# Seven quarter products for eight in a gated linear attention layer, with values and gates of all heads ahead of the heads

## The chip, the core and the metric

The kernel runs on one core of one Trainium2 chip, with nothing on the other cores. The metric is device time in microseconds (us) of one execution, the median of several runs. A core has a matrix engine (TensorE, PE in the profile; its weight loads are PEld), VectorE (DVE), ScalarE (ACT), GpSimd (POOL) and SyncE (SP), each with an instruction queue of its own that works in order, and 16 DMA engines that serve all queues. SBUF is the on-chip memory, PSUM holds TensorE's sums in eight banks of 128 x 512 float32, DRAM lies off the core.

## What is computed

Two layers, each `x <- x + RMSNorm_post(mixer(RMSNorm_pre(x)))`, on 512 tokens of 1024 channels in float32. The first layer (a state-space branch beside a convolution branch) is not touched. The second is gated linear attention with 4 heads, keys of 256 and values of 512 channels a head, in chunks of 64 tokens:

```python
q, k, v, r, lr = jnp.split(u @ od_w_in, ...)          # 1024, 1024, 2048, 2048, 16 columns
g = jax.nn.log_sigmoid(lr @ w_gate_up + b_gate) / 16
b = cumsum of g inside each chunk
attn = where(causal, (q * exp(b)) @ (k * exp(-b)).T, 0)
o = attn @ v + (q * exp(b)) @ state                   # state carried from chunk to chunk
state = exp(b_last) * state + (k * exp(b_last - b)).T @ v
y = (rms_norm(o) * silu(r)) @ od_w_out
```

## The kernel before

**Split numbers.** Every float32 operand of a large product is held as a high part (rounded to TensorE's fp32r) and a low part (the rest), and a product is three matmuls: high x high, low x high, high x low. For weights this is done on the fly: `wlist` names blocks of 128 x 1024 (512 KB) in the order of use; `w_raw` (L113 to L120) loads the next one on SP's queue into one of three `wraw` buffers; `w_split` (L134 to L164) casts it on ScalarE (L155, `wh`, two buffers) and subtracts on VectorE (L161, `wl`, three buffers). In parts of the first layer the low part is made by ScalarE and an accumulating DMA from SBUF to SBUF on GpSimd's queue instead (L130, L131). `w_get` keeps the split one block ahead of its use. `feed()` raises the priority of such work. The order on each engine is made by the planner of the tile framework, which simulates the program with costs of its own and takes what is ready, by priority and then program order.

**A projection with tokens in rows** (`proj_mv`, `mm_mv`, L813 to L831) takes 512 output columns: 4 weight blocks, 4 token groups of 128, 8 groups of 128 channels, 3 matmuls each, 96 matmuls in all, 24 a block (L823 to L825), into four PSUM banks. A head's values are one such projection, its gate r another. Queries and keys go the other way round (`mm_st`, L198 to L201), 24 matmuls a block, 4 blocks a head.

**The second layer.** The normalised input lies in SBUF as `u1h` and `u1l`, 8 channel groups x 512 tokens. First come the values of head 0 (L1003), then the decays of all heads: eight small matmuls (L1006) with absolute value, exponential and logarithm on ScalarE (L1008, L1015), minimum, subtraction and prefix sums on VectorE (L1009, L1024, L1021), then the gate of head 0. Then for each head: queries and keys with their exponentials; values (heads 1 to 3, into the same tiles `vh`, `vl`); scores (L1109) with mask and split into `ah`, `al`; the gate (heads 1 to 3), whose SiLU (L998) stays in SBUF as `rg`; in head 2 also half of the output projection, for heads 0 and 1; then attention times values (L1144 to L1146) for four token groups, each followed by its norm (L1153 to L1156), four transposes (L1159) and a split into `oth`, `otl`. The other half of the output projection and the last norm follow (`proj_tail`).

Of the kernel before, what the change touches and what calls it, by code (L numbers as in the profile page):

```python
# [17 lines left out]
P = 128  # L18
# [33 lines left out]
def trunk(ctx: ExitStack, tc: tile.TileContext, A: dict, out: bass.AP, dbg: dict | None = None):  # L52
# [47 lines left out]
    for n in range(2):  # L100
        for j in range(4):
            wlist.append(A["w_out0"][n, 4 + j])
    for h in range(HEADS):
        wv, wr = ([A["w_vr"][o + h, j] for j in range(4)] for o in (0, 4))
        wqk = [A["w_qk"][2 * h + j] for j in range(2)] + [A["w_qk"][8 + 2 * h + j] for j in range(2)]
        wlist.extend(wv + wr + wqk if h == 0 else wqk + wv + wr)
        if h >= 2:
            for n in range(2):
                for j in range(4):
                    wlist.append((j % 2, A["w_out1"][n, (h - 2) * 4 + j]))  # L110
    wst = {"next_raw": 0, "next_split": 0, "raw": {}, "hl": {}, "low": {}}

    def w_raw():  # L113
        i = wst["next_raw"]
        if i >= len(wlist):
            return
        raw = wpool.tile([P, 1024], F32, tag="wraw", bufs=3, name=f"wraw{i}")
        SY.dma_start(raw, wlist[i][1] if isinstance(wlist[i], tuple) else wlist[i])
        wst["raw"][i] = raw
        wst["next_raw"] = i + 1  # L120
# [13 lines left out]
    def w_split(dst=None):  # L134
        i = wst["next_split"]
        while wst["next_raw"] <= i:
            w_raw()
        if i in dma_low and i not in wst["low"]:
            w_low(i, dst and dst[1])
        raw = wst["raw"].pop(i)  # L140
        h = wpool.tile([P, 1024], F32R, tag="wh", bufs=2, name=f"wh{i}") if dst is None else dst[0]
        if isinstance(wlist[i], tuple):

            l = wpool.tile([P, 1024], F32R, tag="wl", bufs=3, name=f"wl{i}") if dst is None else dst[1]
            for e in range(2):
                es_, g_ = slice(e * S, (e + 1) * S), wst["gain"][:, 2 * wlist[i][0] + e:2 * wlist[i][0] + e + 1]
                with feed():
                    SC.activation(h[:, es_], raw[:, es_], AF.Copy, scale=g_)  # L148
                    V.scalar_tensor_tensor(out=l[:, es_], in0=raw[:, es_], scalar=g_, in1=h[:, es_].bitcast(F32), op0=ALU.mult, op1=ALU.subtract)  # L149
            wst["hl"][i] = (h, l)  # L150
            wst["next_split"] = i + 1
            w_raw()
            return
        with feed():
            SC.copy(h, raw)  # L155
        if i in dma_low:
            l = wst["low"].pop(i)
        else:
            l = wpool.tile([P, 1024], F32R, tag="wl", bufs=3, name=f"wl{i}") if dst is None else dst[1]
            with feed():  # L160
                V.tensor_tensor(out=l, in0=raw, in1=h.bitcast(F32), op=ALU.subtract)  # L161
# [705 lines left out]
    for i in range(2):  # L867
# [7 lines left out]
        wlr.append((wa, wb_))  # L875
    for i in range(2):
        raw = tmp((96, S))
        for r in range(3):
            SY.dma_start(raw[32 * r:32 * r + 32], A["w_gate"][:, i * S:(i + 1) * S])
        g_ = sbt_((96, S), F32R, f"gws{i}")  # L880
        SC.copy(g_, raw)
        V.tensor_sub(g_[64:96], raw[64:96], g_[64:96].bitcast(F32))
        gws.append(g_)
    lrs = sbt_((96, S), F32R, "lrs")

# [78 lines left out]
    wst["gain"] = pa.tile([P, TT], F32, name="ngc")  # L964
    ngp = ps("cv")
    PE.transpose(ngp[:, 0:TT], ngr, ident[0:TT, 0:TT])
    V.tensor_copy(wst["gain"], ngp[:, 0:TT])
    reset = pa.tile([P, S], mybir.dt.bfloat16, name="reset")
# [10 lines left out]
    PG = ExitStack()  # L979
    pg = PG.enter_context(tc.tile_pool(name="l1g", bufs=1, side="right", reuse_waits="tile"))  # L980
    lacc = ps("cv")
    for k in range(KT):
# [9 lines left out]

    def gate(h):
        accs = proj_mv(u1h, u1l)
        rg = []
        for tt in range(TT):
            r_ = sbt_((P, S), F32, f"rg{h}{tt}")
            SC.activation(r_, accs[tt], AF.Silu)  # L998
            rg.append(r_)
        return rg  # L1000

    values(vblocks)
    az = pg.tile([P, KT, S], F32, name="az")  # L1003
    for kt in range(KT):
        gp = ps(("mm", "mm", "mm", "aux", "aux", "aux", "mm", "aux")[kt])
        PE.matmul(gp, gws[kt // 4][:, kt % 4 * P:(kt % 4 + 1) * P], lrs, start=True, stop=True)  # L1006
        bg_ = vec[:, 5, kt:kt + 1]
        SC.activation(az[:, kt, :], gp, AF.Abs, bias=bg_)  # L1008
        V.tensor_scalar(out=bcum[:, kt, :], in0=gp, scalar1=bg_, scalar2=0.0, op0=ALU.add, op1=ALU.min)  # L1009
    last = None  # L1010
    for f, kw in ((AF.Exp, dict(scale=-1.0)), (AF.Ln, dict(bias=1.0))):
        with tc.issue_after(last.ins) if last else ExitStack():
            for k0 in range(0, KT, 2):
                a_ = az[:, k0:k0 + 2, :]
                i_ = SC.activation(a_, a_, f, **kw)  # L1015
        last = i_

# [4 lines left out]

    for kt in range(KT):
        V.tensor_sub(bcum[:, kt, :], bcum[:, kt, :], az[:, kt, :])  # L1024
        if kt == 1:
            sums(0)
    rg = gate(0)
    PG.close()

    pb = L1.enter_context(tc.tile_pool(name="l1b", bufs=1, side="right", reuse_waits="tile"))  # L1030
    pq = LQ.enter_context(tc.tile_pool(name="l1q", bufs=1, side="right", reuse_waits="tile"))
    R_OFF = (0, 448, 768, 960)
# [4 lines left out]
    yp_d = dram.tile([S, D], F32, name="yp_d")  # L1037
    for h in range(HEADS):

# [43 lines left out]
        for j in range(2):  # L1083
# [3 lines left out]
            ec, es = el[j]  # L1087
            evicted = V.tensor_mul(kr[:, 0:S], acc, en[j])  # L1088
            fac = small.tile([P, 3, 2], F32, tag="fac", bufs=2, name=f"fac{h}{j}")
# [3 lines left out]
                            in1=fac.rearrange("p i a -> p (i a)").unsqueeze(2).to_broadcast([P, 6, 64]), op=ALU.mult)  # L1093
            split(kh[:, j, :], kl[:, j, :], kr)
        if h:
# [28 lines left out]
        split(ah[:, 0:S], al[:, 0:S], at.rearrange("p j t -> p (j t)"))  # L1124
        if h:
            rg = gate(h)

        if h == 2:
            for n in range(2):
                accs = proj_mv(*oa)  # L1130
                for tt in range(TT):
                    yt = tmp(name="ypc")
                    SC.copy(yt, accs[tt])
                    SY.dma_start(yp_d[tt * P:(tt + 1) * P, n * S:(n + 1) * S], yt)

        if h % 2 == 0:
            oth = pb.tile([P, KT, S], F32R, tag="oth", bufs=1, name=f"oth{h}")
            otl = bigt(F32R, f"otl{h}")
        acol = {(0, 3): 512, (0, 2): 640, (0, 1): 768, (1, 3): 896, (1, 2): 1024, (2, 3): 1152}
        for i in range(4):  # L1140
            acc = ps("aux")
            for jj in range(i + 1):
                c0 = jj * P if jj == i else acol[(jj, i)]
                PE.matmul(acc, ah[:, c0:c0 + P], vh[:, jj, :], start=(jj == 0), stop=False)  # L1144
                PE.matmul(acc, ah[:, c0:c0 + P], vl[:, jj, :], start=False, stop=False)  # L1145
                PE.matmul(acc, al[:, c0:c0 + P], vh[:, jj, :], start=False, stop=(jj == i))  # L1146
            if "o" in dbg:
# [8 lines left out]
            V.scalar_tensor_tensor(out=og, in0=acc, scalar=rr, in1=rg[i], op0=ALU.mult, op1=ALU.mult)  # L1156
            tp = ps("cv")
            for j in range(4):
                PE.transpose(tp[:, j * P:(j + 1) * P], og[:, j * P:(j + 1) * P], ident)  # L1159
            k0 = 4 * (h % 2)  # L1160
            split(oth[:, k0:k0 + 4, i * P:(i + 1) * P], otl[:, k0:k0 + 4, i * P:(i + 1) * P], tp.rearrange("p (k t) -> p k t", t=P))
        if h == 1:
            oa = (oth, otl)
    LQ.close()

# [11 lines left out]
    E1.close()  # L1177
    L1.close()
    SBP.close()
    L0.close()  # L1180
# [67 lines left out]
```

## Time and profile before

| | |
|---|---|
| median of three runs | 934.77 us (934.74 to 936.48) |
| the profiled execution | 936.94 us, of it 935.2 us span from first to last instruction |
| TensorE busy | 895.1 us, 4397 matmuls, mean granted clock 0.991 |
| VectorE, ScalarE, GpSimd busy | 645.2, 485.1, 225.0 us |
| DMA | 142.48 MB, mean 152 GB/s |
| second layer | from about 520 us on |

A row of the profile names a line of the kernel, an engine, an operation, `out<-in` by tile names, the shapes and the count. "Idle before" is the time in which the engine had nothing to do just ahead of such an instruction, with what ended it. A matmul's shown length is its latency; matmuls overlap, so the distance of their starts is what a stream of them costs. "DMA share" is the mean busy share of the 16 DMA engines, "us to landing" the time from a transfer's issue to its completion.

### The profile page before, as it was taken

Reading aid. Unit: us, or ns where it says so; the run is one execution under the profiler, and the core shown is the slowest. Engines: PE = TensorE matmul, PEld = TensorE weight load, DVE = VectorE, ACT = ScalarE, POOL = GpSimd, SP = SyncE. Lnnn points to the kernel's source line nnn. Section 1 sums busy time; section 2 is a strip of 40 time slices with the busy share of each in tenths; the row PEclk is TensorE's granted clock in tenths of the full one; section 3 lists DMA queues with packets and bytes.
Section 4 is the critical chain, followed back from the end, with each engine's and each line's share of the span. In section 5 each row is a group of like instructions: output and inputs, shape, how many; then the busy total and the mean of one; then the engine's idle time right before and its main releaser. Section 6 shows DMA issues by size and latency. Waiting matters only on the chain. (4 is left out here: it accounts for less than half of the span.)

```text
span 935.2 us, 12132 instructions
## 1 busy us (share of the span) xinstructions
PE 895.1 (96%) x4397; PEld 718.9 (77%) x4397; DVE 645.2 (69%) x1225; ACT 485.1 (52%) x699; POOL 225.0 (24%) x242
## 2 busy tenths in 40 slices
PE   5999998999999999999999979999999999999996
PEld 4876767777788877778887768888888888888885
DVE  7994999999999978822578446694384222744646
ACT  6545686877668745654444654443533243523530
POOL 2795656552041322011054000010000000000022
PEclk9999999999999999999999989999999999999999
DMA  9979987888697894298553122212221223324512
GB/s 288 253 169 228 267 208 181 196 189 203 190 255 203 204 251 135 90 243 186 173 197 113 46 67 96 85 38 77 90 90 68 83 76 136 135 90 152 208 46 90
DMA packets 54820, 142.48 MB, mean 152 GB/s; under 512 B 14245, under 2 KB 15785, under 8 KB 54761
## 3 DMA queue, kind: packets, MB, share of 16 engines
q1 hardware_dynamic: 46696, 112.36, 36.2%
q0 software_dynamic: 8064, 29.36, 17.4%
q8 instruction: 34, 0.56, 0.2%
q14 instruction: 26, 0.20, 0.1%
HBM read 94.92 MB, written 13.22 MB: 116 GB/s over the span
## 5 line engine op out<-in xcount | busy, mean ns | idle before, releaser
L155 ACT CAST wh<-wraw 128x1024 fp32r<-128x1024 f32 x114 | 119.5, 1049 | 138.5 <-PE ps_mm L824 61.9
L676 DVE SCALAR_TENSOR_TENSOR ps_cv<-h,cw,ps_cv 128x512 f32<-128x512 f32 x232 | 161.8, 746 | 2.7 <-ACT ps_cv L673 1.8
L161 DVE TENSOR_TENSOR wl<-wraw,wh 128x1024 fp32r<-128x1024 f32 x58 | 71.6, 1235 | 85.7 <-ACT wh L155 85.7
L198 PE MATMUL ps_mm<-u0h,wh 128*128 128x512 f32 x320 | 128.0, 401 | 1.2 <-ACT tmp L700 0.7
L199 PE MATMUL ps_mm<-u0l,wh 128*128 128x512 f32 x320 | 127.1, 398 | 0.0
L823 PE MATMUL ps_mm<-wh,u1h 128*128 128x512 f32 x240 | 95.6, 400 | 3.3 <-ACT wh L155 3.1
L824 PE MATMUL ps_mm<-wh,u1l 128*128 128x512 f32 x240 | 95.8, 399 | 0.3 <-DVE u1l L206 0.3
L825 PE MATMUL ps_mm<-wl,u1h 128*128 128x512 f32 x240 | 92.6, 402 | 1.7 <-DVE wl L161 1.7
L131 POOL DMA_DIRECT2D wl<-wraw x56 | 48.9, 889 | 172.1 <-ACT wl L130 155.8
L201 PE MATMUL ps_mm<-u0h,wl 128*128 128x512 f32 x320 | 82.4, 396 | 2.2 <-DMA wl<-wraw 2.2
L130 ACT ACTIVATE wl<-wraw 128x1024 fp32r<-128x1024 f32 x56 | 59.2, 1057 | 26.7 <-DMA wraw<-in_w_in_dram 16.2
L198 PEld LDWEIGHTS ps_mm<-u0h,wh 128*128 128x128 f32 x320 | 60.4, 189 | 16.0 <-ACT tmp L700 1.5
L201 PEld LDWEIGHTS ps_mm<-u0h,wl 128*128 128x128 f32 x320 | 59.5, 188 | 16.1 <-DMA wl<-wraw 3.1
L199 PEld LDWEIGHTS ps_mm<-u0l,wh 128*128 128x128 f32 x320 | 60.3, 189 | 13.3 <-issue 0.7
L1092 POOL TENSOR_TENSOR kr<-kr,fac 128x384 f32<-128x384 f32 x8 | 9.1, 1132 | 217.8 <-DVE kr L1088 122.6
L823 PEld LDWEIGHTS ps_mm<-wh,u1h 128*128 128x128 f32 x240 | 45.6, 190 | 14.2 <-ACT wh L155 3.6
L825 PEld LDWEIGHTS ps_mm<-wl,u1h 128*128 128x128 f32 x240 | 45.7, 191 | 13.0 <-DVE wl L161 2.4
L824 PEld LDWEIGHTS ps_mm<-wh,u1l 128*128 128x128 f32 x240 | 45.7, 190 | 11.0 <-DVE u1l L206 0.6
L199 PE MATMUL ps_mm<-u1l,wh 128*128 128x512 f32 x128 | 50.4, 394 | 0.0
L198 PE MATMUL ps_mm<-u1h,wh 128*128 128x512 f32 x128 | 50.3, 393 | 0.0
L149 DVE SCALAR_TENSOR_TENSOR wl<-wraw,ngc,wh 128x512 fp32r<-128x512 f32 x24 | 17.0, 747 | 39.3 <-ACT wh L148 39.3
L903 POOL TENSOR_TENSOR yp<-yp,gain 128x512 f32<-128x512 f32 x8 | 12.6, 1591 | 118.9 <-ACT junk L230 118.9
(348 smaller groups left out, 2041.9 us busy)
## 6 DMA issues: line engine op xcount, KB each, us to landing
wl<-wraw POOLq DMA_DIRECT2D x56, 512.0 KB, 6.4
wraw<-in_w_in_dram SPq DMA_DIRECT2D x40, 512.0 KB, 5.5
wraw<-in_w_out_dram SPq DMA_DIRECT2D x32, 512.0 KB, 3.3
wraw<-in_w_vr_dram SPq DMA_DIRECT2D x32, 512.0 KB, 3.2
wraw<-in_w_qk_dram SPq DMA_DIRECT2D x16, 512.0 KB, 3.2
tm<-kt_d SPq DMA_DIRECT2D x8, 512.0 KB, 7.5
wraw<-in_w_glu_dram SPq DMA_DIRECT2D x8, 512.0 KB, 5.2
wraw<-in_w_pw_dram SPq DMA_DIRECT2D x8, 512.0 KB, 5.3
```

What stands on the lines that cost most here:

```text
L130: SC.activation(l, raw, AF.Copy, scale=-1.0)
L131: G.dma_start(l.bitcast(F32), raw, accum_op=ALU.add)
L149: V.scalar_tensor_tensor(out=l[:, es_], in0=raw[:, es_], scalar=g_, in1=h[:, es_].bitcast(F32), op0=ALU.mult, op1=ALU.subtract)
L155: SC.copy(h, raw)
L161: V.tensor_tensor(out=l, in0=raw, in1=h.bitcast(F32), op=ALU.subtract)
L198: PE.matmul(acc, whv[:, k, :], xh[:, k, :], start=(k == 0), stop=False)
L199: PE.matmul(acc, whv[:, k, :], xl[:, k, :], start=False, stop=False)
L201: PE.matmul(acc, wlv[:, k, :], xh[:, k, :], start=False, stop=(k == KT - 1))
L676: V.scalar_tensor_tensor(out=acc, in0=h[:, k:k + S], scalar=cw[:, c, k:k + 1], in1=acc, op0=ALU.mult, op1=ALU.add)
L823: PE.matmul(accs[tt], xh[:, kt, ts_], whj, start=(first and j == 0), stop=False)
L824: PE.matmul(accs[tt], xl[:, kt, ts_], whj, start=False, stop=False)
L825: PE.matmul(accs[tt], xh[:, kt, ts_], wlj, start=False, stop=(last and j == 1))
```

## The change

For heads 1 to 3 the values and the gate of a head are computed together. The 512 tokens and the 1024 input channels of `u` are halved to four quarters A11, A12, A21, A22; the weights of values (B11 above B21) and of gates (B12 above B22) are halved along the input channels. Seven products of quarters (Winograd's form) replace eight. Each product is 2 weight blocks x 2 token groups x 2 channel groups x 3 matmuls of 512 columns. The four combinations of the input's quarters (S1 to S4) are made once, on GpSimd, and split. The combinations of weights are made by accumulating DMAs on GpSimd's queue that add a block from DRAM onto a block already in SBUF: block i is added onto block i-4 when that one has been split. The products' combinations are made on VectorE and ScalarE as they leave PSUM.

Values (high and low parts) and gates (after SiLU) go to DRAM on SP's queue and come back in the heads' loop, values on GpSimd's queue, gates on SP's. Head 0 is computed as before, except that its gate also goes by DRAM. The order is now: values 0, combinations, gate 0, values and gates 1, the same for 2, queries and keys 0, values and gates 3, then for each head scores, (in head 2) half of the output projection, queries and keys of the next head, attention times values. The decays are cut in pieces that follow the weight blocks of heads 1 and 2: a matmul with its absolute value and minimum behind each of eight blocks of head 1; exponentials, logarithms, subtractions and head 0's prefix sum behind the blocks of head 2, each behind the newest cast on ScalarE and subtraction on VectorE. In attention the transposes of a token group are put behind the matmuls of the second next one, and those of the last two behind all. The score tile is split per token group.

```diff
-        wlist.extend(wv + wr + wqk if h == 0 else wqk + wv + wr)
+        x, add = (lambda w: [("x", w[j]) for j in range(2)]), (lambda w: [("add", w[j]) for j in range(2)])
+        return x(wv[:2]) + wv[2:] + add(wr[:2]) + wr[2:] + add(wr[2:]) + add(wr[:2]) + add(wv[2:])
...
+    for blocks in (vr_blocks(0), vr_blocks(1), vr_blocks(2), qk_blocks(0), vr_blocks(3), qk_blocks(1), qk_blocks(2), out1[0],
+                   qk_blocks(3), out1[1]):
+        wlist.extend(blocks)
...
+        if kind == "add":
+
+            assert i - 4 < wst["next_split"]
+            raw = wst["chain"].pop(i - 4)
+            G.dma_start(raw, src, accum_op=ALU.add)
+        else:
+            raw = (wst["pool"].tile([P, 1024], F32, tag="wx", bufs=3, name=f"wx{i}") if kind == "x" else
+                   wpool.tile([P, 1024], F32, tag="wraw", bufs=3, name=f"wraw{i}"))
+            SY.dma_start(raw, src)
...
+    def gate_low(kt):
+        gp = ps("cv")
         PE.matmul(gp, gws[kt // 4][:, kt % 4 * P:(kt % 4 + 1) * P], lrs, start=True, stop=True)
         bg_ = vec[:, 5, kt:kt + 1]
         SC.activation(az[:, kt, :], gp, AF.Abs, bias=bg_)
         V.tensor_scalar(out=bcum[:, kt, :], in0=gp, scalar1=bg_, scalar2=0.0, op0=ALU.add, op1=ALU.min)
-    last = None
-    for f, kw in ((AF.Exp, dict(scale=-1.0)), (AF.Ln, dict(bias=1.0))):
-        with tc.issue_after(last.ins) if last else ExitStack():
-            for k0 in range(0, KT, 2):
-                a_ = az[:, k0:k0 + 2, :]
-                i_ = SC.activation(a_, a_, f, **kw)
-        last = i_
...
+    def keep_value(h, tt, src):
+        hi, lo = tmp(dt=F32R, name="vhi"), tmp(dt=F32R, name="vlo")
+        split(hi, lo, src)
+        SY.dma_start(vh_d[h][:, tt, :], hi.bitcast(F32))
+        SY.dma_start(vl_d[h][:, tt, :], lo.bitcast(F32))
...
+    def more():
+
+        f = extra.pop(0) if extra else None
+        if f:
+            with tc.issue_after(wst["cast"].ins), tc.issue_after(wst["lowp"].ins):
+                f()
...
+    def product(x):
+
+        accs = [ps("mm" if i_prod[0] % 7 not in (2, 5) else "aux") for _ in range(2)]
+        i_prod[0] += 1
+        for j in range(2):
+            wh, wl = w_get()
+            for tt in range(2):
+                ts_ = slice(tt * P, (tt + 1) * P)
+                for k in range(2):
+                    wk = slice(k * S, (k + 1) * S)
+                    xh, xl = x[0][:, 2 * j + k, ts_], x[1][:, 2 * j + k, ts_]
+                    PE.matmul(accs[tt], xh, wh[:, wk], start=(j == 0 and k == 0), stop=False)
+                    PE.matmul(accs[tt], xl, wh[:, wk], start=False, stop=False)
+                    PE.matmul(accs[tt], xh, wl[:, wk], start=False, stop=(j == 1 and k == 1))
+            more()
+        return accs
...
+        acc = product(A11)
+        u_ = pair_("u")
+        with feed():
+            out_(V, u_, acc, None)
+        acc = product(A12)
+        c11 = [tmp(name="c11") for _ in range(2)]
+        with feed():
+            out_(V, c11, acc, u_)
+        for i in range(2):
+            keep_value(h, i, c11[i])
...
+    extra.extend([lambda kt=kt: gate_low(kt) for kt in range(KT)] + [None] * 6)
+    extra.extend([lambda k0=k0: exp_ln(AF.Exp, k0, scale=-1.0) for k0 in range(0, KT, 2)])
+    extra.extend([lambda k0=k0: exp_ln(AF.Ln, k0, bias=1.0) for k0 in range(0, KT, 2)])
+    extra.extend([lambda: less(0), lambda: sums(0)])
+    extra.extend([lambda k0=k0: less(k0) for k0 in range(2, KT, 2)])
+    values_gate(1)
...
+    values_gate(2)
+    PG.close()
+    pq = LQ.enter_context(tc.tile_pool(name="l1q", bufs=1, side="right", reuse_waits="tile"))
+    queries_keys(0)
+    values_gate(3)
...
         if h:
-            values()
-        if h + 1 < HEADS:
-            with tc.issue_after(evicted.ins):
-                sums(h + 1)
+            G.dma_start(vh, vh_d[h])
+            G.dma_start(vl, vl_d[h])
...
+        if h + 1 < HEADS:
+            queries_keys(h + 1)
```

More of the change, by code (lines that the diff above doesn't have):

```diff
@@ L116, in w_raw @@
             return
-        raw = wpool.tile([P, 1024], F32, tag="wraw", bufs=3, name=f"wraw{i}")
-        SY.dma_start(raw, wlist[i][1] if isinstance(wlist[i], tuple) else wlist[i])
+        kind, src = (wlist[i][0], wlist[i][-1]) if isinstance(wlist[i], tuple) else ("", wlist[i])
+        if kind == "add":
[6 more added lines that the diff above has]
+            SY.dma_start(raw, src)
+        if i + 4 < len(wlist) and isinstance(wlist[i + 4], tuple) and wlist[i + 4][0] == "add":
+            wst["chain"][i] = raw
         wst["raw"][i] = raw
@@ L980, in trunk @@
     pg = PG.enter_context(tc.tile_pool(name="l1g", bufs=1, side="right", reuse_waits="tile"))
+    for i in range(2):
+        raw = tmp((96, S))
+        for r in range(3):
+            SY.dma_start(raw[32 * r:32 * r + 32], A["w_gate"][:, i * S:(i + 1) * S])
+        g_ = pg.tile([96, S], F32R, name=f"gws{i}")
+        SC.copy(g_, raw)
+        V.tensor_sub(g_[64:96], raw[64:96], g_[64:96].bitcast(F32))
+        gws.append(g_)
+    lrs = pg.tile([96, S], F32R, name="lrs")
     lacc = ps("cv")
@@ L1021, in sums @@
             V.tensor_tensor_scan(out=bcum[:, kt, :], data0=reset, data1=bcum[:, kt, :], initial=0.0, op0=ALU.mult, op1=ALU.add)
[L1023 to L1031, printed above, removed]
+    rg_d = [dram.tile([P, TT, S], F32, name=f"rg_d{h}") for h in range(HEADS)]
@@ new lines, in trunk, with keep_gate, gate @@
+    vh_d, vl_d = ([dram.tile([P, TT, S], F32, name=f"v{n}_d{h}") for h in range(HEADS)] for n in "hl")
+    def keep_value(h, tt, src):
[3 more added lines that the diff above has]
+        SY.dma_start(vl_d[h][:, tt, :], lo.bitcast(F32))
+    def keep_gate(h, tt, r_, src):
+        SC.activation(r_, src, AF.Silu)
+        SY.dma_start(rg_d[h][:, tt, :], r_)
+    def gate(h):
+        accs = proj_mv(u1h, u1l)
+        for tt in range(TT):
+            keep_gate(h, tt, sbt_((P, S), F32, f"rg{h}{tt}"), accs[tt])
@@ new lines, in trunk, with quarter @@
+    HT = S // 2
+    LW = ExitStack()
+    pw = LW.enter_context(tc.tile_pool(name="l1w", bufs=1, side="left", reuse_waits="tile"))
+    wst["pool"] = pw
+    s12 = bigt(F32R, "s12")
+    s34 = pw.tile([P, KT, S], F32R, name="s34")
+    def quarter(t, n):
+        q = t.rearrange("p k t -> p (k t)").rearrange("p (q k t) -> p q k t", q=4, t=HT)
+        return q[:, 2 * n], q[:, 2 * n + 1]
+    S1, S2, S3, S4 = quarter(s12, 0), quarter(s12, 1), quarter(s34, 0), quarter(s34, 1)
+    A11, A12, A21, A22 = (tuple(u[:, k:k + 4, t:t + HT] for u in (u1h, u1l)) for t, k in ((0, 0), (0, 4), (HT, 0), (HT, 4)))
@@ new lines, in combos, with part, put, new_ @@
+    def combos():
+        for half in range(2):
+            ks = slice(2 * half, 2 * half + 2)
+            def part(a, n):
+                return a[n][:, ks, :].bitcast(F32)
+            def put(s_, t):
+                SC.copy(s_[0][:, ks, :], t)
+                V.tensor_tensor(out=s_[1][:, ks, :], in0=t, in1=s_[0][:, ks, :].bitcast(F32), op=ALU.subtract)
+            def new_(n):
+                return tmp((P, 2, HT), F32, n)
+            def tt_(o, a, b, op):
+                G.tensor_tensor(out=o, in0=a, in1=b, op=op)
+            t, e = new_("sa"), new_("sb")
+            tt_(t, part(A21, 0), part(A22, 0), ALU.subtract)
+            tt_(e, part(A21, 1), part(A22, 1), ALU.subtract)
+            tt_(t, t, e, ALU.add)
+            put(S1, t)
+            t2_ = new_("sc")
+            tt_(e, part(A11, 0), part(A11, 1), ALU.add)
+            tt_(t2_, t, e, ALU.subtract)
+            put(S2, t2_)
+            t, f = new_("sd"), new_("se")
+            tt_(t, part(A12, 0), part(A12, 1), ALU.add)
+            tt_(t, t2_, t, ALU.add)
+            put(S4, t)
+            tt_(f, part(A21, 0), part(A21, 1), ALU.add)
+            tt_(f, e, f, ALU.subtract)
+            put(S3, f)
@@ new lines, in trunk, with values_gate, pair_, out_ @@
+    i_prod = [0]
+    def values_gate(h):
+        def pair_(n):
+            return [sbt_((P, S), F32, f"{n}{h}{i}") for i in range(2)]
+        def out_(eng, o, a, b, op=ALU.add):
+            for i in range(2):
+                if b is None:
+                    SC.copy(o[i], a[i])
+                else:
+                    eng.tensor_tensor(out=o[i], in0=a[i], in1=b[i], op=op)
+        acc = product(A11)
[6 more added lines that the diff above has]
+            out_(V, c11, acc, u_)
+        for i in range(2):
+            keep_value(h, i, c11[i])
+        acc = product(S1)
+        q5 = pair_("q")
+        with feed():
+            out_(V, q5, acc, None)
+        acc = product(S4)
+        r1 = pair_("r")
+        with feed():
+            out_(V, r1, acc, q5)
+        acc = product(S2)
+        with feed():
+            out_(V, u_, acc, u_)
+        out_(V, r1, r1, u_, ALU.subtract)
+        acc = product(S3)
+        u3 = pair_("v")
+        with feed():
+            out_(V, u3, acc, u_)
+        out_(V, q5, q5, u3, ALU.subtract)
+        for i, r_ in enumerate(r1 + q5):
+            keep_gate(h, i, r_, r_)
+        acc = product(A22)
+        with feed():
+            out_(V, u3, acc, u3)
+        for i in range(2):
+            keep_value(h, 2 + i, u3[i])
@@ L1032, in trunk @@
+    combos()
+    gate(0)
     R_OFF = (0, 448, 768, 960)
@@ L1037, in trunk, with queries_keys @@
     yp_d = dram.tile([S, D], F32, name="yp_d")
-    for h in range(HEADS):
+    qk_of = {}
+    def queries_keys(h):
+        if h:
+            with tc.issue_after(wst["lowp"].ins):
+                sums(h)
         qh = pq.tile([P, 2, NQ], F32R, tag="qh", name=f"qh{h}")
@@ L1156, in trunk @@
             V.scalar_tensor_tensor(out=og, in0=acc, scalar=rr, in1=rg[i], op0=ALU.mult, op1=ALU.mult)
[L1157 to L1161, printed above, removed]
+            ogs.append(og)
+            if i >= 2:
+                with tc.issue_after(last.ins):
+                    turn(i - 2, ogs[i - 2])
+        with tc.issue_after(last.ins):
+            for i in (2, 3):
+                turn(i, ogs[i])
         if h == 1:
             oa = (oth, otl)
+    LB.close()
     LQ.close()
```

85 lines of the change are left out of this document (46 added, 39 removed).

## The prediction, made before the changed kernel was run

> **What bounds the kernel now.** I read the page's engine shares first, then the stages as windows of the second layer, then TensorE's rows in order of time where a window has idle time. On the page:
>
> ```profile
> span 935.2 us, 12132 instructions
> ...
> PE 895.1 (96%) x4397; PEld 718.9 (77%) x4397; DVE 645.2 (69%) x1225; ACT 485.1 (52%) x699; POOL 225.0 (24%) x242
> ```
>
> TensorE is busy 96% of the span, and the next engine, VectorE, 69%. That is a mean over both layers, so the windows decide. Columns: stretch, length, busy time of each engine with its instruction count, granted clock, DMA share, GB/s.
>
> ```profile
> 541.50:552.70 11.20, 6.43 (x18) 4.59 (x18) 8.78 (x12) 4.05 (x5) 0.00 (x0) 0.70 0.20 61
> 560.00:900.00 340.00, 340.00 (x1582) 280.08 (x1581) 181.25 (x426) 140.31 (x223) 10.64 (x11) 1.00 0.29 101
> 912.50:935.20 22.70, 14.33 (x64) 11.53 (x62) 15.08 (x41) 2.17 (x6) 4.71 (x4) 0.92 0.25 92
> ```
>
> From 560 to 900 us TensorE has no idle time at full clock, while VectorE works 53% and the DMA engines 29%. In this stage the time is the number of matmuls times their spacing; whatever else the change moves here is worth nothing until it makes TensorE wait. Only 541.5 to 552.7 is different: 18 matmuls in 11.2 us. The rows of TensorE and of ScalarE there (start, length, instruction, idle time before it and its releaser):
>
> ```profile
> 536.48 0.40 PE L823 MATMUL ps_mm<-wh,u1h 128*128 128x512 f32 x1
> ...
> 541.15 0.39 PE L825 MATMUL ps_mm<-wl,u1h 128*128 128x512 f32 x1
> 544.66 0.50 PE L823 MATMUL ps_mm<-wh,u1h 128*128 128x512 f32 x1 [3.12 <-ACT wh L155]
> ...
> 549.20 2.07 PE L825 MATMUL ps_mm<-wl,u1h 128*128 128x512 f32 x4 [1.65 <-DVE wl L161]
> ...
> 539.77 3.90 ACT L1015 ACTIVATE az<-az 128x1024 f32<-128x1024 f32 x4
> 543.58 1.98 ACT L155 CAST wh<-wraw 128x1024 fp32r<-128x1024 f32 x2
> ```
>
> Between the first two stand 19 more matmuls, so the spacing in a value or gate projection is 4.67 / 20 = 0.2333 us. The stall is gate(0) waiting for its weight block's cast, which stood behind four logarithm passes of the decays; then for the subtraction; and the granted clock was 0.70.
>
> **The change, part by part.** (1) *Fewer matmuls.* A head's values and gates were two projections of 4 blocks x 24 matmuls, 192. In heads 1 to 3 they become seven products of 2 blocks x 12, 168. 3 x 24 x 0.2333 = **16.8 us** less TensorE work. Every product still streams 512 columns, so I take the same spacing. A head now takes 168 x 0.2333 = 39.2 us, and a block 2.8 us where it took 5.6.
>
> (2) *The decays leave gate(0).* At 0.2333 us, 18 matmuls need 4.2 of the 11.2 us: **7.0 us** go with the logarithm passes. What is late next in gate(0) would be the combinations of quarters, which put 8 short copies on ScalarE over some 22 us, between casts, not a block of four; if half the stall stayed it would be 3.5. The Trainium skill, "TensorE: Matmul & The Clock Gate", section "HAM oscillation", says that idle gaps over about 3.4 us drop the clock; here a gap of 3.12 us already went with 0.70, and 7.0 - 3.12 - 1.65 = 2.2 us of the loss is clock.
>
> (3) *Combinations.* 18 GpSimd operations on 128x512, by
>
> ```profile
> L903 POOL TENSOR_TENSOR yp<-yp,gain 128x512 f32<-128x512 f32 x8 | 12.6, 1591 | 118.9 <-ACT junk L230 118.9
> ```
>
> 28.6 us. The last piece of S1 is the twelfth, 19 us after the start, and S1 is first used after gate(0) (96 x 0.2333 = 22.4 us) and the two products on original quarters (11.2). Hidden, at 0; with that cover gone it would be 19. The GpSimd queue holds the first accumulating loads behind them; those are due only in the third product.
>
> (4) *ScalarE and VectorE in the heads.* Rows for casts, subtractions, evictions and the decays' passes:
>
> ```profile
> L155 ACT CAST wh<-wraw 128x1024 fp32r<-128x1024 f32 x114 | 119.5, 1049 | 138.5 <-PE ps_mm L824 61.9
> L161 DVE TENSOR_TENSOR wl<-wraw,wh 128x1024 fp32r<-128x1024 f32 x39 | 47.7, 1224 | 63.2 <-ACT wh L155 63.1
> L206 DVE TENSOR_TENSOR vl<-ps_mm,vh 128x512 fp32r<-128x512 f32 x12 | 8.3, 690 | 5.9 <-ACT vh L205 5.8
> L998 ACT ACTIVATE rg<-ps_mm 128x512 f32<-128x512 f32 x14 | 8.4, 597 | 4.3 <-PE ps_mm L825 3.6
> L1009 DVE TENSOR_SCALAR bcum<-ps_mm,vec 128x512 f32<-128x512 f32 x4 | 2.8, 744 | 1.8 <-ACT az L1008 1.8
> L1024 DVE TENSOR_TENSOR bcum<-bcum,az 128x512 f32<-128x512 f32 x8 | 5.0, 683 | 2.7 <-ACT az L1015 2.7
> L1021 DVE TENSOR_TENSOR_SCAN bcum<-reset,bcum 128x512 f32<-128x512 bf16 x6 | 8.8, 1502 | 0.0
> L1015 ACT ACTIVATE az<-az 128x1024 f32<-128x1024 f32 x8 | 8.0, 1050 | 0.1
> ```
>
> VectorE per head: 14 subtractions x 1.22 + 14 combinations of products x 0.69 + 4 low parts of values x 0.69 = 29.5 us of 39.2. Head 1 adds 8 x 0.74, 35.5. Head 2 adds 8 x 0.68 and two scans of 1.50, **38.0, or 97%**. ScalarE: 14 x 1.05 + 12 x 0.60 = 21.9, with the 8 x 1.05 of head 2 30.3. A block's split (1.05 + 1.22 us) starts when the block two ahead of it is done and must be over in about 2.8 us, and both engines work in order: a piece that stands before a split delays it. The two scans stand together, 3.0 us against 0.5 us of slack. Bounds for the three heads together: 0 (all pieces fit between splits) to 6; I take 3, mostly head 2.
>
> (5) *Accumulating loads.* Eight of a head's 14 blocks are made by adding onto a block in SBUF. The trace has no such load from DRAM; nearest is the addition from SBUF to SBUF in layer 0 (medians from issue to landing, last the spread of the 56, then queue totals):
>
> ```profile
> wl<-wraw POOLq DMA_DIRECT2D x56, 512.0 KB, 6.4
> wraw<-in_w_vr_dram SPq DMA_DIRECT2D x32, 512.0 KB, 3.2
> DMA to landing us min/median/max: 4.5/6.4/11.6
> ...
> q1 hardware_dynamic: 46696, 112.36, 36.2%
> q0 software_dynamic: 8064, 29.36, 17.4%
> ```
>
> Two limits. *Latency:* block j is added onto block j-4 once that is split, so four blocks cost 1.05 + 1.22 + landing; TensorE needs 4 x 2.8 = 11.2 us, so a landing up to 8.9 us is free, and the median 6.4 is well inside. *Throughput:* 17.4% of 935.2 us for 29.36 MB is 5.5 us per MB of all engines; plain transfers 3.0. A head adds 8 x 0.52 = 4.2 MB and moves 6.3 MB plainly (6 block loads; 12 stores of 0.26 for the values' two halves and the gates): 23.1 + 18.9 = 42.0 us against 39.2. With little else in flight plain ones are cheaper:
>
> ```profile
> q1 hardware_dynamic: 1399, 5.08, 70.1%
> ```
>
> in the 19 us from 863, 0.701 x 19 / 5.08 = 2.6 us per MB, giving 39.5. So the DMA engines are about as loaded as TensorE: 0.3 to 2.8 us a head. I take 1.0, nearer the second row, since only loads, stores and adds of this one stage are in flight: **3 us** in all. The stores wait in SP's queue for evictions; loads queued behind them have blocks of lead, 0 within the same bounds.
>
> (6) *Heads' loop.* Values and gates come back from DRAM. For head 3 the two 1 MB loads wait until head 2's last use of vh and vl, and no queries and keys of a next head stand in between.
>
> ```profile
> yp<-yp_d SPq DMA_DIRECT2D x1, 2048.0 KB, 7.9
> ...
> 854.76 0.25 PE L1109 MATMUL ps_aux<-qh,kh 128*128 128x192 f32 x1
> ...
> 856.75 0.41 PE L823 MATMUL ps_mm<-wh,u1h 128*128 128x512 f32 x1
> ...
> 878.62 0.39 PE L823 MATMUL ps_mm<-wh,oth 128*128 128x512 f32 x1
> ...
> 879.21 0.48 PE L1144 MATMUL ps_aux<-vh,ah 128*128 128x512 f32 x1
> ```
>
> 2 MB land in 7.9 us. Scores take 42 matmuls at (856.75 - 854.76) / 18 = 0.11, 4.6 us, which leaves 3.3; and as the last rows show, the planner mixes the output projection into attention times values, with two ready blocks worth 11.2 us. Bounds 0 to 3.3; I take 1. The transposes set behind later matmuls gain nothing where TensorE has no idle time; at the end they may be 1 us either way: 0. The tail after 912.5 keeps its work: 0.
>
> Sum: -16.8 - 7.0 + 3 + 3 + 1 = **-16.8 us**: span 918.4; the profiled execution took 936.94, 1.74 beyond its span, so 920.1. It lies 2.17 above the median 934.77 of the three runs; on that median **918.0 us**. A measurement here can tell about 0.2%, 1.9 us.
>
> **The rivals.** *A, adding costs no more than loading.* The adds then land like the plain loads, 3.2 us, and a head moves 4.2 + 6.3 MB at 3.0 us per MB, 31.5 us of 39.2; (5) vanishes, 915.0, and if the pieces of (4) and the loads of (6) fit as well, 23.8 us stay: 911.0. For it: an add sourced in DRAM reads SBUF once, where layer 0's reads it twice. Against: 6.4 and 5.5 in the rows, and VectorE at 97% in head 2. The Trainium skill, "DMA: Bandwidth & Descriptors", section "Anatomy of one DMA", gives a load issued by GpSimd 2.0 us + bytes / 436 GB/s, which is 3.2 us for 512 KB, and names no surcharge there for adding: by it this rival is the case. The trace agrees with it for plain loads, and not for adds.
>
> *B, the engines' order spoils the heads.* Pieces of the decays, scans, evictions and stores stand before splits more often than I take: each of the 42 blocks loses 0.3 to 0.5 us, 13 to 21 us in place of 6, so 924 to 932. For it: 0.5 us of slack per block. Against: evictions and splits of layer 0 coexist with VectorE nearly full.
>
> *C, slower: accumulating loads from DRAM land late.* The place is the chain of blocks j-4, j. It has three links a head, nine in all. Each link costs landing + 2.3 - 11.2. With 4 us for (4) and (6), level is at 19.8 / 9 = 2.2 us a link, a landing of 11.1 us; that is the point from which it decides. At 11.6, the longest in the trace, a link costs 2.7: 24.3 + 4 - 23.8 = 4.5 us slower, 939; at twice the median, 12.8, 950. For it: source in DRAM, two adds and the stores in flight together, engines nearly full. Against: the median of 6.4 came with layer 0's traffic around it.
>
> That the change does not do what it says can be excluded for the count: products times blocks times 12 is in the code.
>
> **How the numbers follow.** My forecast, 5 to 13 us of new waits (916 to 924), 0.58; A 0.15; B 0.13, of which 0.01 is level and the rest faster by over 0.2%; C 0.14, of which 0.02 is level. Faster 0.58 + 0.15 + 0.12 = 0.85, same 0.03, slower 0.12. The range runs from A's 911 to B's upper end, 932; it leaves out C, 0.14, and a little beyond A and B.
>
> **What would show it.** The changed profile should have 504 matmuls of products spaced 0.233 us; no idle time after a logarithm pass in gate(0); idle time of TensorE in heads 1 to 3 of some 6 us, most in head 2 behind wl's subtraction; adds landing in 5 to 8.9 us; under 3.3 us before head 3's attention times values. I am wrong if TensorE's waits name a cast that waited for an accumulating load (C), if VectorE has room in head 2 and TensorE still waits (B), or if the product matmuls are spaced differently.

## The result and the profile after

The changed kernel takes 921.85 us, median of four runs (921.36 to 923.08), beside 934.75 of the kernel before on the same chip: ratio 0.9861, 95% interval 0.9844 to 0.9878, **12.9 us less** (11.4 to 14.6). The forecast was 16.8 less: the time lies inside the range that was given, 911 to 932, but the gain is smaller than forecast by more than the interval.

The page's first lines, with the profiled execution at 921.64 us:

```profile
span 920.0 us, 12417 instructions
...
PE 878.6 (96%) x4325; PEld 703.9 (77%) x4325; DVE 706.5 (77%) x1305; ACT 511.5 (56%) x746; POOL 277.1 (30%) x290
...
q0 software_dynamic: 12384, 48.24, 27.4%
```

TensorE has 72 matmuls fewer and is busy as large a share; VectorE rose from 69% to 77%. GpSimd's queue moves 48.24 MB where it moved 29.36; of the 18.9 MB more, 12.6 are the 24 accumulating loads and 6.3 the values that come back. The stages (stretch, length, busy of PE, PEld, DVE, ACT, POOL, clock, DMA share, GB/s): the place of the old stall, two pieces of heads 1 and 2, the end of head 2, and the end of the heads' loop.

```profile
541.50:552.70 11.20, 10.77 (x47) 8.41 (x46) 7.93 (x6) 5.91 (x9) 8.04 (x5) 1.00 0.36 125
560.00:580.00 20.00, 20.00 (x88) 16.08 (x87) 13.60 (x17) 11.20 (x14) 5.18 (x6) 1.00 1.01 234
600.00:620.00 20.00, 20.00 (x87) 15.83 (x86) 13.61 (x17) 16.61 (x20) 5.17 (x6) 1.00 1.01 258
620.00:640.00 20.00, 17.26 (x72) 13.11 (x71) 17.96 (x33) 14.43 (x18) 0.00 (x0) 1.00 0.70 191
862.00:880.00 18.00, 15.55 (x81) 12.60 (x79) 14.18 (x44) 10.03 (x24) 0.00 (x0) 1.00 0.73 261
```

Where 18 matmuls stood in 11.2 us there are now 47. In heads 1 and 2 the DMA engines are full (a share of 1.01, so packets overlap) and TensorE still has no idle time; it has some at the end of head 2 and at the end of the loop. TensorE's waits from 449 us on (total, times, longest) name both:

```profile
PE ps_cv L1328 <- DVE vv L239: 2.0, 1, 2.0
PE ps_aux L1120 <- DVE wl L179: 1.4, 1, 1.4
PE ps_mm L842 <- DVE u1l L224: 1.3, 1, 1.3
PE ps_mm L216 <- ACT wh L173: 0.9, 1, 0.9
PE ps_aux L266 <- DVE xg L262: 0.8, 1, 0.8
PE ps_mm L1120 <- DVE wl L179: 0.5, 1, 0.5
PE ps_mm L926 <- DVE yp L910: 0.5, 1, 0.5
PE ps_mm L843 <- DVE wl L179: 0.4, 1, 0.4
PE ps_mm L841 <- ACT wh L173: 0.3, 1, 0.3
```

In none of them does TensorE wait for a cast whose block was still being added. The second is a weight block's subtraction in head 2. VectorE's rows there, with the casts ahead:

```profile
619.72 1.05 ACT L173 CAST wh<-wraw 128x1024 fp32r<-128x1024 f32 x1 [2.93 <-DMA wraw<-in_w_vr_dram]
...
620.80 1.23 DVE L179 TENSOR_TENSOR wl<-wraw,wh 128x1024 fp32r<-128x1024 f32 x1 [1.55 <-ACT wh L173]
621.95 2.33 DVE L1021 TENSOR_TENSOR_SCAN bcum<-reset,bcum 128x512 f32<-128x512 bf16 x2
...
622.13 1.05 ACT L173 CAST wh<-wraw 128x1024 fp32r<-128x1024 f32 x1 [1.36 <-DVE wl L179]
...
624.20 1.26 DVE L1135 TENSOR_TENSOR u<-ps_mm,u 128x512 f32<-128x512 f32 x2
...
625.38 1.22 DVE L179 TENSOR_TENSOR wl<-wraw,wh 128x1024 fp32r<-128x1024 f32 x1
...
626.65 0.50 PE L1120 MATMUL ps_aux<-wl,s 128*128 128x512 f32 x1 [1.39 <-DVE wl L179]
```

The first cast waited 2.93 us for its accumulating load, so its subtraction starts only at 620.80, and the two scans stand behind that. The second cast is done at 623.2, but the scans and two combinations stand ahead of its subtraction, which starts at 625.4.

**A measure with less chance in it.** Up to 447 us both kernels run the same instructions in the same order on every engine, yet the last matmul of the first layer's branch (on xbl) starts anywhere from 444.9 to 448.9 us in the profiles of this document. So the experiments are also compared by the *stretch* from there to the end of the last matmul: before 478.1 us, after 462.5.

### The profile page after: what moved, and what is told of

Its sections match the earlier page's. It is cut to its first block, busy times and chain, and to the rows that moved or that the text cites. A ratio compares the mean times of both kernels' runs of the same rounds, so it can differ in the third digit from the quotient of the medians.

```text
span 920.0 us, 12417 instructions
## 1 busy us (share of the span) xinstructions
PE 878.6 (96%) x4325; PEld 703.9 (77%) x4325; DVE 706.5 (77%) x1305; ACT 511.5 (56%) x746; POOL 277.1 (30%) x290
## 3 DMA queue, kind: packets, MB, share of 16 engines
q0 software_dynamic: 12384, 48.24, 27.4%
## 4 chain that ended last, share of the span: by engine, by line
PE 56%; DVE 18%; issue 8%; DMA 7%; POOL 6%; ACT 4%; SPq 1%; DVEq 0%; ACTq 0%; POOLq 0%
PE ps_mm L216 9%; PE ps_mm L217 9%; PE ps_mm L219 9%; DVE ps_cv L694 5%; PE ps_mm L843 4%; PE ps_mm L842 4%; PE ps_mm L841 4%; PE ps_aux L1289 2%; PE ps_mm L1120 1%; PE ps_mm L1119 1%; PE ps_mm L1118 1%; DMA wraw<-in_w_vr_dram 1%; DMA yp<-yp_d 1%; DMA wraw<-in_w_out_dram 1%; DVE zb L647 1%
## 5 line engine op out<-in xcount | busy, mean ns | idle before, releaser
L173 ACT CAST wh<-wraw 128x1024 fp32r<-128x1024 f32 x108 | 113.2, 1048 | 105.5 <-PE ps_mm L217 62.0
L179 DVE TENSOR_TENSOR wl<-wraw,wh 128x1024 fp32r<-128x1024 f32 x52 | 69.4, 1337 | 39.0 <-ACT wh L173 38.3
L130 POOL DMA_DIRECT2D wx<-in_w_vr_dram x18 | 15.6, 866 | 98.5 <-DVE wl L179 96.6
L179 DVE TENSOR_TENSOR wl<-wx,wh 128x1024 fp32r<-128x1024 f32 x24 | 29.4, 1224 | 14.8 <-ACT wh L173 14.8
L173 ACT CAST wh<-wx 128x1024 fp32r<-128x1024 f32 x24 | 25.2, 1048 | 26.9 <-PE ps_mm L1119 13.4
L842 PE MATMUL ps_mm<-wh,otl 128*128 128x512 f32 x96 | 38.4, 400 | 0.0
L841 PE MATMUL ps_mm<-wh,oth 128*128 128x512 f32 x96 | 37.8, 397 | 0.0
L843 PE MATMUL ps_mm<-wl,oth 128*128 128x512 f32 x96 | 37.6, 395 | 0.0
L219 PE MATMUL ps_mm<-u1h,wl 128*128 128x512 f32 x128 | 32.7, 396 | 0.0
```

Source lines behind the costliest of these rows:

```text
L173: wst["cast"] = SC.copy(h, raw)
L179: wst["lowp"] = V.tensor_tensor(out=l, in0=raw, in1=h.bitcast(F32), op=ALU.subtract)
L219: PE.matmul(acc, wlv[:, k, :], xh[:, k, :], start=False, stop=(k == KT - 1))
L841: PE.matmul(accs[tt], xh[:, kt, ts_], whj, start=(first and j == 0), stop=False)
L842: PE.matmul(accs[tt], xl[:, kt, ts_], whj, start=False, stop=False)
L843: PE.matmul(accs[tt], xh[:, kt, ts_], wlj, start=False, stop=(last and j == 1))
```

## The experiments

**1. Does the first profile repeat?** The kernel before, unchanged.

> The kernel before, profiled once more, to see how much of its first profile repeats. The first profiled execution took 936.94 us, 2.2 above the median. Theory: the stall in gate(0) repeats in full (idle 3.1 us before a cast and 1.7 us before a subtraction, because the instruction order is fixed), but the drop of the granted clock behind it (2.2 us of loss) need not, so the span is 932.5 to 935.5. Rival: the stall itself is a matter of one execution; then TensorE's waits list no cast of 3 us.

935.79 us, span 934.1, stretch 477.7:

```profile
PE ps_mm L823 <- ACT wh L155: 3.1, 1, 3.1
PE ps_mm L825 <- DVE wl L161: 1.4, 1, 1.4
```

The stall in gate(0) repeats, and the stretch within 0.4 us. The slow clock behind the stall, which I had left open, repeats too: 0.83 from 540 to 560 us in both profiles.

**2. Eight products in the new order.**

```diff
-        return x(wv[:2]) + wv[2:] + add(wr[:2]) + wr[2:] + add(wr[2:]) + add(wr[:2]) + add(wv[2:])
+        return wv + wr
...
-        acc = product(A11)
...
+        for n in range(2):
+            accs = [ps("mm") for _ in range(TT)]
+            for j in range(4):
+                mm_mv(accs, w_get(), u1h, u1l, 0, 2 * j, j == 0, j == 3)
+                for _ in range(1 if h == 1 else 2):
+                    more()
```

> The changed kernel with the usual eight products: values and gates of heads 1 to 3 as two projections of 4 blocks x 24 matmuls each, no combinations, no accumulating loads; the new order, the decays in pieces and the way through DRAM stay. Theory (the gain is the 72 matmuls, 16.8 us, less about 4 us of waits that the seven products bring): 930 to 935 us, that is 0.995 to 1.000 of before. Rival (order and decays bring the gain, the seven products pay back what they save in splits, adds and VectorE's time): 921 to 924 us, as the changed kernel.

932.69 us, ratio 0.9986 (0.9973 to 1.0000), stretch 473.9. By the stretch 10 us of the gain belong to the seven products (473.9 - 463.7, the mean of the changed kernel's two below), by the ratios 12 (0.0125 of 934); order and decays together bring only 1 to 4. The time came out as my theory had it. Order and decays bring less than the stall of 7 us, for this kernel has longer waits elsewhere, as the changed kernel has:

```profile
PE ps_cv L1288 <- DVE vv L236: 1.8, 1, 1.8
PE ps_mm L839 <- DVE u1l L221: 1.3, 1, 1.3
```

The first is the wait at the end of the heads' loop. The second, at the start of the values of head 0, was 0.3 us in the kernel before, and not every profile of the changed kernel has it (run 5 has none).

**3. Adds made copies.**

```diff
-            G.dma_start(raw, src, accum_op=ALU.add)
+            G.dma_start(raw, src)
```

> The changed kernel with the 24 accumulating loads made plain copies of the same block into the same buffer, from the same queue and behind the same waits, so that heads 1 to 3 multiply by other weights. Theory (the adds land at 8.3 us in the median, just inside the 8.9 that are free, and nothing waits): 921 to 922.5 us, the same as the changed kernel, though the copies land 2 us or more earlier and the DMA engines fall from full to some 80%. Rival (the adds and the full DMA engines hold the heads back): 917 to 919 us.

918.97 us, ratio 0.9841 (0.9821 to 0.9862), stretch 462.3. The time lies in the rival's range, not in that of my theory. In heads 1 and 2 of the changed kernel, then of this one (KB each, median us to landing):

```profile
q0 software_dynamic: 2304, 8.39, 57.0%
...
wx<-in_w_vr_dram POOLq DMA_DIRECT2D x12, 512.0 KB, 7.8
wraw<-in_w_vr_dram POOLq DMA_DIRECT2D x4, 512.0 KB, 8.7
```

```profile
q0 software_dynamic: 2304, 8.39, 32.3%
...
wx<-in_w_vr_dram POOLq DMA_DIRECT2D x12, 512.0 KB, 4.2
wraw<-in_w_vr_dram POOLq DMA_DIRECT2D x4, 512.0 KB, 4.9
```

The same bytes from DRAM to SBUF take 57.0% of the engines' time when they add and 32.3% when they copy, and land 3.6 us later. What that is worth to TensorE is small and not settled: 1.0 or 1.9 us by the ratio, set against the changed kernel's two measurements (0.9852 and 0.9861), whose intervals overlap this one, and 0.2 or 2.5 us by the stretch. One wait did shrink, the 1.4 us of head 2 to 0.2: no cast of these heads waits for a load any more, so the scans are over sooner. The late add had a part in that wait.

**4. The kernel before without the decays' passes.**

```diff
-            for k0 in range(0, KT, 2):
-                a_ = az[:, k0:k0 + 2, :]
-                i_ = SC.activation(a_, a_, f, **kw)
```

> The kernel before without the exponential and logarithm passes of the decays (eight ScalarE passes and their two table loads left out, so the decays are others). Theory (they alone make the stall in gate(0)): 927.5 to 930.5 us, 4.8 to 7.0 less than before, 0.9925 to 0.995. Rival (the subtractions on VectorE or the weight blocks would be late next): under 2 us less, 933 or more.

926.61 us, ratio 0.9926 (0.9906 to 0.9946), 6.9 us less; stretch 470.0, 7.9 less than the mean of the two profiles before. Nothing was late next.

**5. The changed kernel again.** No edit.

> The changed kernel once more, timed beside before in five rounds. Up to 447 us both kernels have the same instructions in the same order on every engine, yet that stretch differed by some 4 us between profiles; from the last matmul on xbl (448.7 us before, 448.9 after) to the last matmul of all before took 478.1 us and the changed kernel 462.5. Theory (the stretch that the change touches is 15.4 us shorter, and what the medians lack of it is the first layer's chance): the ratio comes out at 0.983 to 0.987, and the stretch is again 462.0 to 463.0 us. Rival (the change slows the first layer by some 2.5 us): 0.986 or more, with the first stretch long in this profile too.

921.11 us, ratio 0.9852 (0.9830 to 0.9874). The stretch was 464.8, outside what I expected, though TensorE's waits sum to 7.4 us, 0.7 less than in the first profile. The granted clock was lower in two places where the first profile had 1.00, and 65 x 0.03 = 2.0 and 18 x 0.09 = 1.6 us make up for the 2.3 + 0.7 us, roughly:

```profile
445.00:510.00 65.00, 63.32 (x280) 51.49 (x279) 47.60 (x99) 28.56 (x50) 22.18 (x16) 0.97 0.48 162
...
860.00:878.00 18.00, 16.03 (x75) 13.07 (x75) 13.51 (x42) 9.63 (x23) 0.00 (x0) 0.91 0.75 271
```

In the first place it was 0.83 from 490 to 500 us, behind a wait of 1.6 us for the norm between the layers; in the second it fell behind the loop's last wait, 2.0 us. So a stretch repeats to some 2 us; its mean, 463.7, is 14.2 below the mean before, 477.9. The first part was short here (446.4), so the change does not slow the first layer.

**6. One link of two blocks.** The product of S4 moves ahead of that of S1, so that blocks 8 and 9 are added onto 6 and 7. ScalarE makes two more copies a head, since both products now leave PSUM before they are added.

```diff
-        return x(wv[:2]) + wv[2:] + add(wr[:2]) + wr[2:] + add(wr[2:]) + add(wr[:2]) + add(wv[2:])
+        return x(wv[:2]) + wv[2:] + wr[2:] + add(wr[:2], 6) + add(wr[2:], 2) + add(wr[:2], 6) + add(wv[2:], 4)
```

> The changed kernel with the products in another order, so that one add of each head (blocks 8 and 9) goes onto the block two ahead of it in place of four; the others have four or six. The adds, bytes, splits and matmuls are as many. Theory (the chain costs split + landing = 2.3 + 8.3 us, and is free only where four blocks, 11.2 us, cover it): two blocks are 5.6 us, so TensorE waits 3 to 5 us a head for a cast behind an accumulating load, and the stretch from the last matmul on xbl grows by 9 to 15 us, to 471 to 478; 929 to 937 us. Rival (blocks are made far enough ahead, no such chain): no wait on an accumulating load, within 2 us of the changed kernel.

938.31 us, ratio 1.0036 (1.0020 to 1.0052): slower than before. The stretch is 480.3, beyond the 478 of my theory, which had left out the clock. TensorE's longest wait, the chain in head 2, and the windows around the waits of the three heads:

```profile
PE ps_mm L1120 <- ACT wh L175: 11.4, 4, 4.4
```

```profile
613.50 1.23 DVE L181 TENSOR_TENSOR wl<-wx,wh 128x1024 fp32r<-128x1024 f32 x1
...
615.01 0.86 POOL L131 DMA_DIRECT2D wx<-in_w_vr_dram  x1 [3.48 <-DVE wl L181]
...
622.96 1.04 ACT L175 CAST wh<-wx 128x1024 fp32r<-128x1024 f32 x1 [5.69 <-DMA wx<-in_w_vr_dram]
...
624.05 0.50 PE L1120 MATMUL ps_mm<-wh,s 128*128 128x512 f32 x1 [4.36 <-ACT wh L175]
```

```profile
570.00:585.00 15.00, 11.25 (x43) 8.74 (x42) 6.86 (x10) 5.60 (x7) 2.28 (x3) 0.89 0.82 165
615.00:632.00 17.00, 12.64 (x48) 9.73 (x47) 8.62 (x10) 7.96 (x10) 3.45 (x4) 0.90 0.87 184
686.00:700.00 14.00, 10.87 (x41) 8.39 (x40) 5.63 (x7) 4.12 (x6) 2.57 (x3) 0.88 0.88 172
```

Subtraction, add, cast and matmul follow each other: the subtraction ends at 614.73, the add is issued at 615.01 and lands 7.8 us later, at 622.86, and the cast starts at 622.96. So this link costs 1.05 + 1.22 + 7.8 = 10.1 us where two blocks of matmuls last 5.6: 4.5 us, and TensorE waits 4.4 (3.75 and 3.13 in the other two heads). 11.4 us are waits; the clock takes up to 15 x 0.11 + 17 x 0.10 + 14 x 0.12 = 5.0 in these windows. Together some 16.4, and the stretch grew by 16.6 against the changed kernel's mean.

**7. The scans apart.**

```diff
-    extra.extend([lambda: less(0), lambda: sums(0)])
+    extra.extend([lambda: less(0)] + [lambda kt=kt: V.tensor_tensor_scan(out=bcum[:, kt, :], data0=reset, data1=bcum[:, kt, :], initial=0.0, op0=ALU.mult, op1=ALU.add) for kt in range(2)])
```

> The changed kernel with head 0's two prefix scans behind two different blocks of head 2 in place of one. Theory (the wait of 1.4 us in head 2 is the two scans that stand together ahead of a subtraction): it goes, the stretch from the last matmul on xbl to the last matmul is 1 to 1.5 us shorter, 461 to 461.5. Rival (VectorE has no room in head 2, 97%): the wait turns up at another block, 462 to 463.

917.55 us, ratio 0.9818 (0.9797 to 0.9838), stretch 460.3, a little below what I expected. The wait of 1.4 us is one of 0.5, and that of 0.9 at the end of head 2 is gone:

```profile
PE ps_cv L1328 <- DVE vv L239: 1.8, 1, 1.8
PE ps_mm L842 <- DVE u1l L224: 1.3, 1, 1.3
PE ps_aux L266 <- DVE xg L262: 1.2, 1, 1.2
PE ps_aux L1120 <- DVE wl L179: 0.5, 1, 0.5
```

It is the fastest version, 17 us below the kernel before. Its 95% interval overlaps by a little with that of the changed kernel measured beside it (0.9830 to 0.9874); the waits that went, 1.8 us, are the surer part.

**8. Transposes behind all matmuls in the last head**, with the scans apart.

```diff
-            if i >= 2:
+            if i >= 2 and h < 3:
...
-            for i in (2, 3):
+            for i in (2, 3) if h < 3 else range(4):
```

> As the run before, and in the last head the transposes of all four token groups stand behind the last attention matmul. Theory (the wait of 2.0 us ahead of the first transposes is the norm's chain of token group 0, and 2.8 us of matmuls of group 3 can cover it): it goes, the stretch is 2 us shorter again, 459 to 459.5, unless the output projection then waits for the transposed groups. Rival (the projection's third block is next in line and waits as long): 461 to 461.5.

920.35 us, ratio 0.9849 (0.9825 to 0.9872), stretch 461.4. A miss: the wait only changed its place.

```profile
PE ps_aux L1336 <- DVE vv L239: 1.8, 1, 1.8
...
PE ps_mm L841 <- ACT oth L223: 0.7, 1, 0.7
```

Now the matmuls of group 3 wait for the same norm. They need a PSUM bank, the kernel has three of that kind, and the first is held until group 0 is normalised. So the wait is for the norm, whatever stands next in line. The second row is new: the output projection now waits 0.7 us for a transposed group, the case that I had left open.

**9. Head 2 without the decays' pieces.**

```diff
-    extra.extend([lambda k0=k0: exp_ln(AF.Exp, k0, scale=-1.0) for k0 in range(0, KT, 2)])
-    extra.extend([lambda k0=k0: exp_ln(AF.Ln, k0, bias=1.0) for k0 in range(0, KT, 2)])
-    extra.extend([lambda: less(0), lambda: sums(0)])
-    extra.extend([lambda k0=k0: less(k0) for k0 in range(2, KT, 2)])
```

> The changed kernel without the exponentials, logarithms, subtractions and first prefix sums that stand behind head 2's weight blocks (the decays are others; heads 1 to 3 keep their prefix sums). It prices them together. From the last matmul on xbl to the end of the last matmul the changed kernel took 462.5 and 464.8 us in two profiles. Theory (two scans ahead of one subtraction are all that they cost; the other pieces fit between splits): the wait of 1.4 us goes and the stretch is 460.5 to 461.5, as with the scans apart. Rival (the pieces cost ScalarE or VectorE time all through head 2, 0.3 us and more a block): 457 to 459.5.

920.50 us, ratio 0.9831 (0.9793 to 0.9869), stretch 465.1. Both expectations missed. No wait on a subtraction is left in head 2, but the planner now puts four exponentials, two table loads and a SiLU ahead of the first query block's cast:

```profile
PE ps_mm L216 <- ACT wh L173: 2.8, 1, 2.8
```

With less to do, another order, and 1.9 us more of waiting at that place. The clock was lower as well, 0.98 from 551 to 638 us and from 800 to 880 (1.00 in the changed kernel's first profile), some 3.3 us. So this run cannot price the pieces: what it took out and what the new order and the clock put in stand against each other, and by the ratio it is not slower than the changed kernel.

**10. Head 3's values not reloaded.**

```diff
-        if h:
+        if 0 < h < 3:
             G.dma_start(vh, vh_d[h])
             G.dma_start(vl, vl_d[h])
```

> The changed kernel without the reload of head 3's values (head 3 multiplies by head 2's, which lie in SBUF). In the changed kernel 47 matmuls of the output projection fill the time in which these 2 MB arrive, and none are left when attention of head 3 waits for its norms. Theory: attention of head 3 starts some 11 us earlier, the projection's matmuls come after its first groups as they did before the change, and the wait of 2.0 us before the first transposes goes: stretch 460 to 461, 2 us less. Rival (the wait is the chain of the norm and three PSUM banks alone, whatever comes first): 462 to 464.8, with the wait in place.

920.89 us, ratio 0.9831 (0.9790 to 0.9872), stretch 462.5. The attention of head 3 starts where it did (866.73 us; 866.56 in the changed kernel), with 48 matmuls of the output projection ahead of it, and the waits are cut up, not gone:

```profile
PE ps_aux L1336 <- ACT at L1296: 1.1, 1, 1.1
...
PE ps_cv L1328 <- DVE vv L239: 0.3, 1, 0.3
```

My theory for this run fell: the projection's matmuls stand among the scores of head 3 with the loads or without them. No time is seen that the loads cost.

## Why the prediction was right, and where it was not

The direction and the order of the sum held: TensorE's instructions set the time, and taking 72 away pays, less some waits.

(1) *16.8 us of matmuls.* The products' blocks start 2.80 us apart in head 1, as worked out (3.04 where a small matmul of the decays stands between). By run 2 the seven products are worth 10 to 12 net. (2) *7.0 us of stall.* 6.9 by the ratio of run 4. (3) *Combinations at 0.* GpSimd's work itself is hidden, but gate(0) has two short waits, 0.3 us for a cast and 0.4 for a subtraction, each behind a combination's copy or subtraction; run 2, without combinations, has neither. (4) and (5), *6 us in the heads*, came out at 2.8 (1.4 + 0.9 + 0.5 in the waits), in head 2 alone. The reason given, two scans together ahead of a subtraction, holds for the 1.4: apart, they leave 0.5 (run 7). But the add that landed late has a part in it as well: without it 0.2 are left (run 3). The share that I worked out for VectorE in head 2, 97%, was too high for the head as a whole and too low for its end:

```profile
591.40:632.90 41.50, 39.63 (x168) 30.85 (x166) 32.00 (x40) 32.02 (x37) 6.90 (x8) 1.00 0.95 233
...
620.80:634.00 13.20, 10.59 (x44) 7.63 (x42) 13.20 (x17) 8.26 (x10) 0.00 (x0) 1.00 0.85 230
```

Over the head it is 32.0 of 41.5 us, 77%: rows of one engine overlap by a little, and some pieces came later. From 620.80 on VectorE has no idle time at all, and all three waits lie there. The mean hides this; which pieces pile up at the end, behind a split that started late, decides. For (5) the 24 adds landed in 5.3 to 10.0 us, median 8.3, inside the 8.9 that I gave as free but for six of them, with the DMA engines full as forecast; run 3 puts what that cost at 0.2 to 2.5 us.

(6) is the step that failed. It forecast 1 us for the values' reload in head 3, because "the planner mixes the output projection into attention times values". In run 10, without the reload of head 3, attention starts no earlier, so that wait did not come. What came instead is a wait of 2.0 us for the norm of token group 0. In the kernel before, matmuls of gate(3) stood among the scores of head 3 and, 48 of them from 863.75 us on, beside the first matmuls of its attention, and none of the projection's 96 matmuls stood ahead of that. With all gates ahead of the heads, 48 of them cover the scores, and none stands beside the attention's first norms. Run 2 has this wait (1.8 us) with eight products, so it belongs to the order, not to the products. That the lost cover is the cause is read from the order of the instructions in the two traces; no run gave the cover back. This is the cover that I named for (6) and did not follow one step further: who used it before.

The size: the stretch fell by 15.6 us in the first pair of profiles and by 14.2 in the mean of two and two, against 16.8 in the sum. In the first pair TensorE's waits went from 6.9 us to 8.1, 1.2 more, where the sum had 2.2 more; matmuls and waits alone make 15.6. That this is the measured number is partly luck, for the sum also took 2.2 us of slow clock out of gate(0), and the changed kernel's first profile has none in its place. Other losses, which the sum left out, make up for it. A listed wait counts from the end of a matmul's row, which is 0.39 us long while starts are 0.23 apart, so each wait costs some 0.16 us more than listed (from 624.87 to 626.65 us the starts are 1.78 apart, 1.55 more than usual, where the row says 1.39); with nine waits in place of five that is 0.6 us. The 393 matmuls of queries and keys, with the last nine on xbl, take 91.4 us by the distance of their starts where they took 90.7, 0.7 more. The rest, about 1 us, stays open. In the second profile the clock came back in the two places of run 5, which is why the mean is lower. The waits that came where the sum had none (gate(0), the start of the second layer, the output projection) also hide that (4) and (5) together were put 3 us too high.

The rivals. *C* was right as a mechanism, and run 6 shows its point: where a link is shorter than split plus landing, TensorE waits, the clock falls, and the change is slower than before. At four blocks a link it does not come to that, but it is near: casts on ScalarE waited 12.8 us for adds, in six places, and one of them is behind the wait of 1.4. *A* was wrong in its reason: adding costs 1.8 times the engines' time of copying, and a load issued by GpSimd lands in 4.2 us if it copies and in 7.8 if it adds. The Trainium skill, "DMA: Bandwidth & Descriptors", section "Anatomy of one DMA", gives 2.0 us + bytes / 436 GB/s for a load issued by GpSimd, an estimate of 3.2 us for 512 KB, and does not tell adds from copies; the copies of run 3 are nearer to it than the adds. (The plain loads of 3.2 us in the prediction's row were SP's.) *B* did not come at its size: in heads 1 and 3 the waits list no block. In head 2 its mechanism is there, at 2.8 us.

## What to carry to other kernels

Where TensorE is without idle time, count its instructions first; then look not at an engine's mean share but at the stretch where it is full, and at what stands ahead of each split in its queue, and keep added pieces shorter than the split's slack. A chain through DMA is free while its links are longer than split plus landing: here 11.2 us covered 2.3 + 8.3, and 5.6 against 2.3 + 7.8 cost some 16 in three heads, 11.4 of waits and the rest of clock. When cover is moved, ask what it hid at its old place and what must now hide that.

## What the runs showed of the hardware

Accumulating 512 KB loads from DRAM took 57.0 / 32.3 = 1.8 times the DMA engines' time of plain ones from the same queue. The granted clock fell after waits of 3.1 to 4.4 us (0.70 in the gate(0) window, 0.88 to 0.90 in the windows of run 6). After shorter ones it fell in some profiles and not in others: behind the loop's wait of 2.0 us it was 0.91 over 18 us in run 5 and 1.00 in the changed kernel's first profile, and behind a wait of 1.6 us for the norm between the layers 0.83 over 10 us in run 5 and 1.00 in the kernel before. The Trainium skill, "TensorE: Matmul & The Clock Gate", section "HAM oscillation", puts the limit at about 3.4 us of idle time; here shorter waits went with a lower clock as well. An unchanged first part of 447 us differed by 4 us from run to run, which is more than most of the terms of the sum.
